# A hybrid encoder layer: the residual branch computed during attention and parked in DRAM

## The chip, the cores and the metric

The kernel runs on one core of one Trainium2 chip. The metric is the device time of one execution in microseconds, lower being better. The core's engines are named as in the profile: PE (matrix multiply), PEld (its weight loads), DVE (vector), ACT (activation), POOL (GpSimd) and SP (the engine that here issues DMAs).

## The reference, cut to what matters

One encoder layer over 1024 tokens of width 1024. The input is layer-normalised, projected by a 1024 x 6688 matrix, and read by two parallel groups: a bidirectional state-space scan (16 heads) and a differential attention (8 heads, two softmax maps each). Both outputs go through one output projection, and the normalised input is added back:

```python
h = layer_norm(x, ln_emb_g, ln_emb_b)
proj = h @ w_in                       # z, xbc, dt, q, k, v, g
...                                   # y_ssm from z, xbc, dt;  y_attn from q, k, v, g
mix = concatenate([y_ssm, y_attn]) @ w_out
out = layer_norm(ALPHA * h + mix, ln_g, ln_b)
```

The change is about the term `ALPHA * h`, called the residual or skip path below. Everything is float32; products are made from split high and low parts, three matmuls for one.

## The kernel before, in words

The program is one long straight line, woven by a planner (`Loom`, L47) from generators called lanes. Each lane yields what it must wait for; the planner keeps an estimate of each engine's time and, at each step, resumes the lane that could go first, ties being decided by the rank in `LANES` (L29). The order of the PE's instructions is fixed by that weave. The framework under it places the instructions of the other engines, each engine being an in-order queue.

The stages, by time in the profile: up to 90 us the input is normalised and transposed; to 450 us the state-space groups run beside the input projection; to about 1000 us the eight heads run (`scores`, `combine`, `values`, `finish`) while the rest of the input projection fills the PE (`fill`); the last head then runs beside the first half of the output projection (`project_out`, part 0), and from about 1110 us only the output projection, the final normalisation and the stores are left.

Names that the change and the prediction touch:

- `values` (L1033) writes each half head's output into the tile `o`, two buffers; `finish` (L1070) normalises and gates it and stores it to DRAM.
- `combine` (L1016) makes the map `p0*rs + p1*rs'`: a scaling on POOL (on ACT for the last head), then one two-input DVE instruction, listed as `p<-p,rs,p`.
- `rows_out` (L1137) loads row tiles `ws` of `w_out` and splits them into `oh`/`or` (ACT) and `ol`/`or` (POOL and DVE in turn).
- `y_out` (L1167) reads the concatenated outputs back as `ys` and splits them into `oyh` (ACT) and `oyl` (DVE).
- `residuals` (L1189) starts once the pool `ow` is open, after the projections of the last head. For each of 8 token tiles and 2 halves it loads `x` into `xr` and runs one ACT and two POOL instructions on it, plus one small `nmr` on DVE for each token tile.
- `project_out` (L1245) adds the residual to its PSUM banks (`bk`), which it shares with the transposes of `values`.
- `z_block` (L466) and `proj_k` (L909) each end in a DMA issued from SP: `zd<-zs` (16 times) and `kk<-kk` (32 times).

Of the kernel before, what the change touches and what calls it, by code (L numbers as in the profile page):

```python
# [9 lines left out]
F32 = mybir.dt.float32  # L10
# [9 lines left out]
D = 1024  # L20
# [5 lines left out]
EPS = 1e-5  # L26
ALPHA = 2.0 ** 0.25

LANES = dict(weights=(0, 0.8), channels=(1, 1.2), steps=(2, 1.6), z_tail=(2, 0.8), conv=(3, 1), v_tail=(3, 0.4), states=(4.4, 0.8), diag=(4.125, 0.6), maps=(4.4, 0.6), gate=(4.375, 0.2), finish=(4.2, 2), scores=(4, 0.8), combine=(4.125, 0.6), values=(4.25, 0.4), fill=(9, 0.8), rows_out=(9, 0.2), y_out=(9, 3), residuals=(9, 2), project_out=(9, 2))  # L29


def col_bcast(ap, n):
# [184 lines left out]
def hybrid_layer_kernel(  # L217
# [13 lines left out]
    VO = Engine(loom, nc.vector, "DVE", _dve_cost, pinned=True)  # L231
    AO = Engine(loom, nc.scalar, "ACT", _act_cost, pinned=True)
    SP = Engine(loom, nc.sync, "DMA", _dma_cost)
    x, out = x[0], out[0]
    w_in, w_out, conv_w = w_in[0], w_out[0], conv_w[0]

# [12 lines left out]

    def dma(dst, src):  # L250
        SP.dma_start(dst, src)

    def transpose(dst, src, n=128):
        T.transpose(dst, src, ident[:n, :n])
# [109 lines left out]
    y_dram = [dr.tile([128, 16, 128], F32, name=f"yd{k}") for k in range(8)]  # L364
    acs_dr = [dr.tile([16, NCH, 128], F32, name=f"acs_d{d}") for d in range(2)]
    zd = [dr.tile([NCH, 128, 512], F32, name=f"zd{g}") for g in range(2)]


    g0x = px.enter_context(ExitStack())
# [96 lines left out]
    def z_block(g, j, when=None):  # L466
        def evac(half, ps):
            zr = late["sq"].tile([128, 512], F32, name="zr", bufs=2)
            A.copy(zr, ps)

            def tail():
                pt = bank((128, 4, 128))
                yield (zr, pt)
                for i in range(4):
                    transpose(pt[:, i, :], zr[:, 128 * i:128 * i + 128])
                zs = late["sq"].tile([128, 4, 128], F32, name="zs", tag="zr", bufs=2)
                A.activation(zs, pt, AF.Silu)
                dma(zd[g][4 * half:4 * half + 4, :, 128 * j:128 * j + 128].rearrange("c p n -> p c n"), zs)
                G[g].z_done += 1
            loom.add(tail(), "z_tail")  # L480
        queue.append(Block(Z0 + 512 * g + 128 * j, evac, when))
# [427 lines left out]
    def proj_k(h):  # L909
        H = heads_[h]  # L910

        def evac(half, ps):
            if half == 0:
                H.kk = H.pool().tile([128, 2, S], F32R, name="kk")
                H.kl = H.pool().tile([128, S], F32R, name="kl")
            t = slice(512 * half, 512 * half + 512)
            for m in range(2):
                a, b = slice(64 * m, 64 * m + 64), slice(64 - 64 * m, 128 - 64 * m)
                A.copy(H.kk[a, m, t], ps[a])
                V.tensor_sub(H.kl[a, t], ps[a], H.kk[a, m, t].bitcast(F32))  # L920
                dma(H.kk[b, m, t].bitcast(F32), H.kk[a, m, t].bitcast(F32))
            H.k += 1
        queue.append(Block(K0 + 128 * h, evac, free_since(h, "scored", 8)))

# [108 lines left out]
    def values():  # L1033

        for _ in range(64):
            yield lambda: bool(maps_)
            H, tb, w = maps_.pop(0)
            if tb % 2 == 0:
                wh = ap.tile([128, NCH, 256], F32R, name="wh")
                wl = ap.tile([128, NCH, 256], F32R, name="wl")  # L1040
            t = slice(128 * (tb % 2), 128 * (tb % 2) + 128)
            for half in range(2):
                pt = bank((128, 4, 128))
                yield (w, pt)
                for j in range(4):
                    s = 4 * half + j
                    transpose(pt[:, j, :], w[:, 128 * s:128 * s + 128])
                b = slice(4 * half, 4 * half + 4)
                A.copy(wh[:, b, t], pt)
                yield wh  # L1050
                V.tensor_sub(wl[:, b, t], pt, wh[:, b, t].bitcast(F32))
            count["t"] += 1
            if tb % 2 == 0:
                continue
            yield lambda: H.v == 2
            if tb % 4 == 1:
                H.o = ap.tile([128, 512], F32, name="o", bufs=2)
            po = bank()
            yield (wl, H.vl, po)
            for s in range(NCH):  # L1060
                T.matmul(po[:, 0:256], H.vh[:, s, :], wh[:, s, :], start=(s == 0), stop=False)
                T.matmul(po[:, 0:256], H.vh[:, s, :], wl[:, s, :], start=False, stop=False)
                T.matmul(po[:, 0:256], H.vl[:, s, :], wh[:, s, :], start=False, stop=(s == NCH - 1))
            n = tb // 2 % 2
            A.copy(H.o[:, 256 * n:256 * n + 256], po[:, 0:256])
            H.summed += 1
            if n:
                loom.add(finish(H, H.o, tb // 4))
# [32 lines left out]
    for h in range(1, 8):  # L1101
        project_head(h)
    queue[-2].pair = queue[-1].last = True
    for lane in (scores, combine, values):
        loom.add(lane())


# [29 lines left out]
    def rows_out():  # L1137

        yield lambda: h_used[0] > 0
        order = [(k, n) for k in range(16) for n in range(2)]  # L1140
        sts = []

        def load():
            k, n = order[len(sts)]
            sts.append(ap.tile([128, 512], F32, name="ws", bufs=10))
            dma(sts[-1], w_out[128 * k:128 * k + 128, 512 * n:512 * n + 512])
        for _ in range(10):
            load()
        for places in (early_rows(), late_rows()):
            for p in places:  # L1150
                if callable(p):
                    yield p
                    continue
                k, n = order[sum(len(w) for w in wo)]
                st, (hi, lo) = sts[2 * k + n], p
                A.copy(hi, st)
                (V if n else P).tensor_sub(lo, st, hi.bitcast(F32))
                wo[k].append(p)
                if len(sts) < 32:
                    load()  # L1160
                if sum(len(w) for w in wo) == 32:
                    return
# [4 lines left out]
    def y_out():  # L1167

        for tb, part in units:
            if part == 0:  # L1170
                yield lambda: h_used[1] > 0 and len(ahead) < 2
            else:
                yield lambda: last.done == 2 and len(ahead) < 2
            parts = []
            for i in range(2):
                st = wp.tile([128, 4, 128], F32, name="ys", tag="wst", bufs=2)
                dma(st, y_dram[tb][:, 8 * part + 4 * i:8 * part + 4 * i + 4, :])
                hi = wp.tile([128, 4, 128], F32R, name="oyh", tag="whi", bufs=4)
                lo = wp.tile([128, 4, 128], F32R, name="oyl", tag="wlo", bufs=4)
                A.copy(hi, st)  # L1180
                V.tensor_sub(lo, st, hi.bitcast(F32))
                parts.append((hi, lo))
            ahead[tb, part] = parts

    res = {}
    used = set()
    halves = [slice(0, 512), slice(512, 1024)]

    def residuals():  # L1189

        yield lambda: "pool" in res
        for n, src in (("g", ln_emb_g), ("b", ln_emb_b)):
            res[n] = res["pool"].tile([128, D], F32, name=n + "_e")
            dma(res[n], src.partition_broadcast(128))
            A.activation(res[n], res[n], AF.Copy, scale=ALPHA)
        late = [("zr", 2), ("zr", 2), ("o", 2), ("o", 2), ("osq", 1), ("msq", 1)]
        for tb in range(8):
            yield lambda: tb < len(used) + 2 or tb > NE
            if tb == NE:
# [1 line left out]
            if tb > NE:  # L1201
                yield lambda: last.done == 2
            xr = []
            nmr = ap.tile([128, 1], F32, name="nmr", bufs=2)
            V.scalar_tensor_tensor(nmr, mv[tb][:, 0:1], -1.0, rstd[tb], op0=ALU.mult, op1=ALU.mult)
            for n, t in enumerate(halves):
                if tb < NE:
                    xr.append(res["pool"].tile([128, 512], F32, name=f"xr{tb}_{n}"))
                else:
                    tag, bufs = late[2 * (tb - NE) + n]  # L1210
                    xr.append(ap.tile([128, 512], F32, name="xr", tag=tag, bufs=bufs))
                dma(xr[n], x[128 * tb:128 * tb + 128, t])
                A.activation(xr[n], xr[n], AF.Identity, scale=rstd[tb], bias=nmr)
                P.tensor_mul(xr[n], xr[n], res["g"][:, t])
                P.tensor_add(xr[n], xr[n], res["b"][:, t])
            res[tb] = xr
        for n, src in (("g", ln_g[0]), ("b", ln_b[0])):
            res[n + "o"] = res["pool"].tile([128, D], F32, name=n + "_o", tag=n + "_e")
            dma(res[n + "o"], src.partition_broadcast(128))

    def norm_out(tb, xr, po, final):
        st = ap.tile([128, 2, 6], F32, name="bst", bufs=2)
# [96 lines left out]
```

## Time and profile before

| | us |
|---|---|
| median of 3 runs (1234.08 to 1236.62) | 1236.25 |
| the profiled execution, its own time | 1231.77 |
| its span, first to last instruction | 1230.1 |
| PE busy in the span | 1173.1 |

All times of rows are microseconds from the start of the span unless marked ns. A busy time is the union of an engine's instructions; the bracket at the end of a timeline line is the idle time before it and what ended it. Nearly all instructions show line L140, a helper's, so they are told apart by the names of tiles: `p<-p,rs,p` writes `p` and reads `p`, `rs` and `p`.

### The profile page before, as it was taken

Reading aid. Unit: us, or ns where it says so; the run is one execution under the profiler, and the core shown is the slowest. Engines: PE = TensorE matmul, PEld = TensorE weight load, DVE = VectorE, ACT = ScalarE, POOL = GpSimd, SP = SyncE. Lnnn points to the kernel's source line nnn. Section 1 sums busy time; section 2 is a strip of 40 time slices with the busy share of each in tenths; the row PEclk is TensorE's granted clock in tenths of the full one; section 3 lists DMA queues with packets and bytes.
Section 4 is the critical chain, followed back from the end, with each engine's and each line's share of the span. In section 5 each row is a group of like instructions: output and inputs, shape, how many; then the busy total and the mean of one; then the engine's idle time right before and its main releaser. Section 6 shows DMA issues by size and latency. Waiting matters only on the chain. (4 is left out here: it accounts for less than half of the span.)

```text
span 1230.1 us, 16472 instructions
## 1 busy us (share of the span) xinstructions
PE 1173.1 (95%) x5881; PEld 920.5 (75%) x5881; DVE 898.5 (73%) x1303; ACT 701.8 (57%) x1281; POOL 471.2 (38%) x404
## 2 busy tenths in 40 slices
PE   5999999999999999999999999999999997999997
PEld 3777667788668777778787777877777776788885
DVE  6686876767876568788788887887878888762334
ACT  4557578734577466566655657556656686552221
POOL 7412564323753223323332333233232429352354
PEclk9999999999899999999999999999999999999999
DMA  6113345622344531111111121121111263023221
GB/s 199 30 36 112 86 129 158 185 64 65 94 122 144 153 113 43 28 47 48 26 48 39 43 53 26 35 52 36 43 35 43 79 210 116 26 77 121 78 86 60
DMA packets 107590, 98.02 MB, mean 80 GB/s; under 512 B 9364, under 2 KB 79349, under 8 KB 107509
## 3 DMA queue, kind: packets, MB, share of 16 engines
q1 hardware_dynamic: 107509, 96.98, 27.4%
q8 instruction: 46, 0.75, 0.3%
q14 instruction: 35, 0.29, 0.1%
HBM read 75.85 MB, written 16.91 MB: 75 GB/s over the span
## 5 line engine op out<-in xcount | busy, mean ns | idle before, releaser
L140 PE MATMUL bk<-hh,whi 128*128 128x512 f32 x832 | 352.8, 424 | 0.9 <-DVE yt L140 0.3
L140 PE MATMUL bk<-hl,whi 128*128 128x512 f32 x832 | 327.2, 393 | 3.2 <-POOL hl L140 2.8
L140 PE MATMUL bk<-hh,wlo 128*128 128x512 f32 x832 | 328.2, 394 | 0.0
L140 ACT ACTIVATE p<-p,nm 128x1024 f32<-128x1024 f32 x128 | 146.8, 1148 | 127.7 <-DVE nm L140 126.9
L140 POOL TENSOR_TENSOR wlo<-wst,whi 128x512 fp32r<-128x512 f32 x104 | 159.0, 1534 | 144.6 <-ACT whi L140 122.2
L140 POOL TENSOR_SCALAR p<-p,rs 128x1024 f32<-128x1024 f32 x56 | 64.4, 1150 | 352.7 <-DVE rs L140 293.0
L140 PEld LDWEIGHTS bk<-hh,wlo 128*128 128x128 f32 x832 | 156.7, 188 | 35.0
L140 PEld LDWEIGHTS bk<-hh,whi 128*128 128x128 f32 x832 | 157.6, 189 | 33.1 <-issue 5.7
L140 PEld LDWEIGHTS bk<-hl,whi 128*128 128x128 f32 x832 | 157.8, 190 | 32.8 <-POOL hl L140 5.5
L140 DVE CUSTOM_DVE_ANT_0 p<-sc,dist 128x1024 f32<-128x1024 f32 x128 | 151.3, 1219 | 20.2 <-PE sc L140 19.6
L140 DVE SCALAR_TENSOR_TENSOR p<-p,rs,p 128x1024 f32<-128x1024 f32 x64 | 127.7, 1995 | 21.3 <-POOL p L140 18.0
L140 ACT CAST wh<-bk 128x512 fp32r<-128x512 f32 x128 | 74.2, 580 | 50.5 <-PE bk L140 49.9
L140 DVE TENSOR_TENSOR wl<-bk,wh 128x512 fp32r<-128x512 f32 x128 | 87.1, 684 | 15.6 <-ACT wh L140 13.6
L140 ACT CAST whi<-wst 128x512 fp32r<-128x512 f32 x104 | 64.1, 621 | 42.5 <-PE bk L140 34.3
L140 PE MATMUL bk<-ident,p 128*128 128x128 f32 x512 | 78.3, 275 | 2.6 <-ACT o L140 2.2
L140 PEld LDWEIGHTS bk<-ident,p 128*128 128x128 f32 x512 | 61.0, 140 | 26.1 <-issue 5.5
L140 ACT ACT_TABLE_LOAD x46 | 59.0, 1283 | 28.9 <-DVE t L140 17.3
L140 PE MATMUL bk<-wh,vh 128*128 128x256 f32 x256 | 74.7, 292 | 0.0
L140 PE MATMUL sc<-kk,q 128*128 128x512 f32 x256 | 72.3, 394 | 0.0
L140 PE MATMUL bk<-wl,vh 128*128 128x256 f32 x256 | 72.0, 281 | 0.0
L140 PE MATMUL bk<-wh,vl 128*128 128x256 f32 x256 | 72.0, 281 | 0.0
L140 PEld LDWEIGHTS bk<-xt,t 128*128 128x128 f32 x256 | 45.0, 190 | 24.7 <-issue 16.0
(217 smaller groups left out, 2161.3 us busy)
## 6 DMA issues: line engine op xcount, KB each, us to landing
wst<-in_w_in_dram SPq DMA_DIRECT2D x104, 256.0 KB, 3.0
t<-acs_d SPq DMA_DIRECT2D x64, 256.0 KB, 3.4
ws<-in_w_out_dram SPq DMA_DIRECT2D x32, 256.0 KB, 3.8
ys<-yd SPq DMA_DIRECT2D x32, 256.0 KB, 3.0
xb<-in_x_dram SPq DMA_DIRECT2D x8, 512.0 KB, 6.5
zd<-zs SPq DMA_DIRECT2D x16, 256.0 KB, 3.0
gz<-zd SPq DMA_DIRECT2D x16, 256.0 KB, 3.1
yd<-ys SPq DMA_DIRECT2D x16, 256.0 KB, 2.8
```

Source lines behind the costliest of these rows:

```text
L140: r = f(*args, **kw)
```

## The change

- A new lane `skip_rows` computes the residual during attention. It runs a burst after each of eight half heads (the second to the ninth `o` tile). A burst has two tiles of 128 x 512: load `x`, one small DVE instruction, one ACT instruction, two on POOL, and, delayed by two tiles, a store to the new DRAM tensor `xr_dram`. The tiles are taken from the ring of `o`, which grows from two to four buffers. The scale and bias are loaded by halves.
- `residuals` now only loads `xr_dram` and, first, the last norm's scale and bias.
- `ws` goes from ten buffers to seven.
- For part 0, the first of the two `oyl` subtractions goes from DVE to POOL (8 instructions).
- The DMAs `zd<-zs` and `kk<-kk` are issued from ACT's queue in place of SP's.

```diff
-LANES = dict(... scores=(4, 0.8), ...)
+LANES = dict(... skip_rows=(3.9, 0), scores=(4, 0.8), ...)
...
+    AD = Engine(loom, nc.scalar, "DMA", _dma_cost)
+    def dma_act(dst, src):
+        AD.dma_start(dst, src)
+    xr_dram = [dr.tile([128, D], F32, name=f"xrd{b}") for b in range(NCH)]
...
-                dma(zd[g][4 * half:4 * half + 4, :, 128 * j:128 * j + 128].rearrange("c p n -> p c n"), zs)
+                dma_act(zd[g][4 * half:4 * half + 4, :, 128 * j:128 * j + 128].rearrange("c p n -> p c n"), zs)
...
-                dma(H.kk[b, m, t].bitcast(F32), H.kk[a, m, t].bitcast(F32))
+                dma_act(H.kk[b, m, t].bitcast(F32), H.kk[a, m, t].bitcast(F32))
...
-                H.o = ap.tile([128, 512], F32, name="o", bufs=2)
+                H.o = ap.tile([128, 512], F32, name="o", bufs=4)
+                o_turn[0] += 1
...
+    def skip_rows():
+        left = []
+        def store():
+            dst, t = left.pop(0)
+            dma(dst, t)
+        for i in range(8):
+            yield lambda: o_turn[0] > i + 1
+            for j in range(2):
+                n, tb = i // 4, 2 * (i % 4) + j
+                t = slice(512 * n, 512 * n + 512)
+                if tb == 0:
+                    for name, src in (("g", ln_emb_g), ("b", ln_emb_b)):
+                        resid[name] = ap.tile([128, 512], F32, name=name + "_e")
+                        dma(resid[name], src[t].partition_broadcast(128))
+                        A.activation(resid[name], resid[name], AF.Copy, scale=ALPHA)
+                if len(left) > 1:
+                    store()
+                xe = ap.tile([128, 512], F32, name="xe", tag="o", bufs=4)
+                dma(xe, x[128 * tb:128 * tb + 128, t])
+                nmr = ap.tile([128, 1], F32, name="nmr", bufs=2)
+                V.scalar_tensor_tensor(nmr, mv[tb][:, 0:1], -1.0, rstd[tb], op0=ALU.mult, op1=ALU.mult)
+                A.activation(xe, xe, AF.Identity, scale=rstd[tb], bias=nmr)
+                P.tensor_mul(xe, xe, resid["g"])
+                P.tensor_add(xe, xe, resid["b"])
+                left.append((xr_dram[tb][:, t], xe))
+        while left:
+            store()
...
-            sts.append(ap.tile([128, 512], F32, name="ws", bufs=10))
+            sts.append(ap.tile([128, 512], F32, name="ws", bufs=7))
...
-                V.tensor_sub(lo, st, hi.bitcast(F32))
+                (V if part or i else P).tensor_sub(lo, st, hi.bitcast(F32))
...
-            nmr = ap.tile([128, 1], F32, name="nmr", bufs=2)
-            V.scalar_tensor_tensor(nmr, mv[tb][:, 0:1], -1.0, rstd[tb], op0=ALU.mult, op1=ALU.mult)
...
-                dma(xr[n], x[128 * tb:128 * tb + 128, t])
-                A.activation(xr[n], xr[n], AF.Identity, scale=rstd[tb], bias=nmr)
-                P.tensor_mul(xr[n], xr[n], res["g"][:, t])
-                P.tensor_add(xr[n], xr[n], res["b"][:, t])
+                dma(xr[n], xr_dram[tb][:, t])
```

## Rows read from the trace of the kernel before

**Rows 1.** The page's first part: busy us, share of the span, instructions.
```profile
PE 1173.1 (95%) x5881; PEld 920.5 (75%) x5881; DVE 898.5 (73%) x1303; ACT 701.8 (57%) x1281; POOL 471.2 (38%) x404
```
**Rows 2.** Windows: length, busy PE, PEld, DVE, ACT, POOL, then clock, DMA share, GB/s.
```profile
90.00:450.00 360.00, 340.83 (x1613) 261.80 (x1612) 257.99 (x335) 221.33 (x473) 148.33 (x132) 0.99 0.41 121
490.00:770.00 280.00, 278.90 (x1503) 220.09 (x1502) 224.87 (x338) 174.05 (x303) 85.92 (x64) 1.00 0.16 39
1000.00:1065.00 65.00, 57.65 (x280) 45.44 (x279) 52.48 (x71) 45.88 (x73) 44.03 (x31) 0.95 0.39 127
...
1110.00:1222.00 112.00, 112.00 (x484) 90.61 (x482) 37.79 (x72) 22.31 (x33) 46.96 (x39) 1.00 0.28 86
```
**Rows 3.** Timeline of PE from 1000 to 1065: the matmuls after idle time.
```profile
1020.22 0.50 PE L140 MATMUL bk<-oh,oyh 128*128 128x512 f32 x1 [2.47 <-DVE wl L140]
1040.71 1.39 PE L140 MATMUL bk<-oh,oyh 128*128 128x512 f32 x2 [3.91 <-DVE wl L140]
1064.23 0.50 PE L140 MATMUL bk<-oh,oyh 128*128 128x512 f32 x1 [0.97 <-DVE xr L140]
```
**Rows 4.** Windows, columns as in rows 2, behind the second gap.
```profile
1040.70:1042.00 1.30, 1.28 (x3) 0.89 (x4) 1.30 (x3) 0.00 (x0) 1.22 (x2) 0.50 0.00 0
...
1046.00:1048.00 2.00, 2.00 (x9) 1.09 (x8) 0.00 (x0) 0.00 (x0) 2.00 (x2) 0.86 0.00 0
```
**Rows 5.** Timeline of DVE ahead of the first gap's end.
```profile
1015.36 2.40 DVE L140 TENSOR_TENSOR oyl<-ys,oyh 128x512 fp32r<-128x512 f32 x2
...
1018.34 1.22 DVE L140 TENSOR_TENSOR rs<-rs,neg_lam 128x1 f32<-128x1 f32 x1
1019.48 0.68 DVE L140 TENSOR_TENSOR wl<-bk,wh 128x512 fp32r<-128x512 f32 x1
```
**Rows 6.** Timelines of ACT and of DVE ahead of the second gap's end.
```profile
1035.91 2.91 ACT L140 ACTIVATE xr<-xr,nmr,rstd 128x512 f32<-128x512 f32 x4
1038.73 0.56 ACT L140 CAST wh<-bk 128x512 fp32r<-128x512 f32 x1
...
1036.56 2.28 DVE L140 SCALAR_TENSOR_TENSOR p<-p,rs,p 128x1024 f32<-128x1024 f32 x1
1038.77 1.29 DVE L140 SCALAR_TENSOR_TENSOR nmr<-mv,rstd 128x1 f32<-128x1 f32 x2
1039.98 0.68 DVE L140 TENSOR_TENSOR wl<-bk,wh 128x512 fp32r<-128x512 f32 x1
```
**Rows 7.** Tile xr: duration ns min/median/max, first and last start us, forms.
```profile
L140 ACT ACTIVATE xr<-xr,nmr,rstd x16: 798/808/819, 1017.3 to 1119.5; 128x512 f32<-128x512 f32 x16
L140 POOL TENSOR_TENSOR xr<-xr,g_e x16: 1266/1298/2279, 1018.2 to 1120.4; 128x512 f32<-128x512 f32 x16
L140 POOL TENSOR_TENSOR xr<-xr,b_e x16: 1278/1298/2123, 1019.6 to 1121.8; 128x512 f32<-128x512 f32 x16
```
**Rows 8.** Windows of tile xr alone: length, busy DVE, ACT, POOL, clock, DMA.
```profile
1000.00:1065.00 65.00, 3.70 (x6) 8.87 (x12) 34.41 (x24) 0.95 0.39 127
```
**Rows 9.** Tiles rs, p, oyl, o and ws, columns as in rows 7.
```profile
L140 DVE TENSOR_TENSOR rs<-rs,neg_lam x64: 151/160/1223, 436.5 to 1082.8; 128x1 f32<-128x1 f32 x64
L140 DVE SCALAR_TENSOR_TENSOR p<-p,rs,p x64: 1268/2296/2340, 437.8 to 1085.8; 128x1024 f32<-128x1024 f32 x64
...
L140 DVE TENSOR_TENSOR oyl<-ys,oyh x32: 676/684/1795, 990.7 to 1200.3; 128x512 fp32r<-128x512 f32 x32
...
L140 ACT COPY o<-bk x32: 346/352/373, 460.8 to 1098.5; 128x256 f32<-128x256 f32 x32
...
L140 ACT CAST oh<-ws x16: 617/622/637, 971.2 to 1012.8; 128x512 fp32r<-128x512 f32 x16
```
**Rows 10.** Tiles zs and kk: the DMA issues, columns as in rows 7.
```profile
L140 SPq DMA_DIRECT2D zd<-zs x16: 359/371/508, 122.4 to 388.3; - x16
...
L140 SPq DMA_DIRECT2D kk<-kk x32: 461/467/777, 406.3 to 964.3; - x32
```
**Rows 11.** Waits of SP's queue, 90 to 450: us in total, times, longest.
```profile
SPq L140 <- ACT zs L140: 27.0, 11, 7.1
```

More of the change, by code (lines that the diff above doesn't have):

```diff
@@ L27 @@
 ALPHA = 2.0 ** 0.25
-LANES = dict(weights=(0, 0.8), channels=(1, 1.2), steps=(2, 1.6), z_tail=(2, 0.8), conv=(3, 1), v_tail=(3, 0.4), states=(4.4, 0.8), diag=(4.125, 0.6), maps=(4.4, 0.6), gate=(4.375, 0.2), finish=(4.2, 2), scores=(4, 0.8), combine=(4.125, 0.6), values=(4.25, 0.4), fill=(9, 0.8), rows_out=(9, 0.2), y_out=(9, 3), residuals=(9, 2), project_out=(9, 2))
+LANES = dict(weights=(0, 0.8), channels=(1, 1.2), steps=(2, 1.6), z_tail=(2, 0.8), conv=(3, 1), v_tail=(3, 0.4), states=(4.4, 0.8), diag=(4.125, 0.6), maps=(4.4, 0.6), gate=(4.375, 0.2), finish=(4.2, 2), skip_rows=(3.9, 0), scores=(4, 0.8), combine=(4.125, 0.6), values=(4.25, 0.4), fill=(9, 0.8), rows_out=(9, 0.2), y_out=(9, 3), residuals=(9, 2), project_out=(9, 2))
 def col_bcast(ap, n):
@@ L1103, in hybrid_layer_kernel @@
     queue[-2].pair = queue[-1].last = True
-    for lane in (scores, combine, values):
+    resid = {}
+    o_turn = [0]
+    def skip_rows():
[25 more added lines that the diff above has]
+            store()
+    res = {}
+    for lane in (scores, combine, values, skip_rows):
         loom.add(lane())
@@ L1144, in load @@
             k, n = order[len(sts)]
-            sts.append(ap.tile([128, 512], F32, name="ws", bufs=10))
+            sts.append(ap.tile([128, 512], F32, name="ws", bufs=7))
             dma(sts[-1], w_out[128 * k:128 * k + 128, 512 * n:512 * n + 512])
-        for _ in range(10):
+        for _ in range(7):
             load()
@@ L1180, in y_out @@
                 A.copy(hi, st)
-                V.tensor_sub(lo, st, hi.bitcast(F32))
+                (V if part or i else P).tensor_sub(lo, st, hi.bitcast(F32))
                 parts.append((hi, lo))
             ahead[tb, part] = parts
-    res = {}
     used = set()
@@ L1191, in residuals @@
         yield lambda: "pool" in res
[L1192 to L1196, printed above, removed]
+        for n, src in (("g", ln_g[0]), ("b", ln_b[0])):
+            res[n + "o"] = res["pool"].tile([128, D], F32, name=n + "_o")
+            dma(res[n + "o"], src.partition_broadcast(128))
+        late = [("zr", 2), ("zr", 2), ("o", 4), ("o", 4), ("o", 4), ("o", 4)]
         for tb in range(8):
@@ L1211, in residuals @@
                     xr.append(ap.tile([128, 512], F32, name="xr", tag=tag, bufs=bufs))
-                dma(xr[n], x[128 * tb:128 * tb + 128, t])
-                A.activation(xr[n], xr[n], AF.Identity, scale=rstd[tb], bias=nmr)
-                P.tensor_mul(xr[n], xr[n], res["g"][:, t])
-                P.tensor_add(xr[n], xr[n], res["b"][:, t])
+                dma(xr[n], xr_dram[tb][:, t])
             res[tb] = xr
-        for n, src in (("g", ln_g[0]), ("b", ln_b[0])):
-            res[n + "o"] = res["pool"].tile([128, D], F32, name=n + "_o", tag=n + "_e")
-            dma(res[n + "o"], src.partition_broadcast(128))
     def norm_out(tb, xr, po, final):
```

## The prediction

> **What bounds the kernel now.** I read the page's first part first: PE is busy 95% of the span [rows 1], so only PE's idle time and a lower clock can be won back: the change takes no matmul away. Then windows by stage [rows 2]. In 490 to 770, attention with projections filling in, PE is busy 278.90 of 280 us, while DVE has 224.87, ACT 174.05 and POOL 85.92: there is room beside PE, most of it on POOL. In 1110 to 1222, where the output projection stands alone, PE is busy 112.00 of 112: nothing done for the other engines there can pay. In 1000 to 1065, the last head beside the output projection, PE is busy 57.65 of 65 and its clock averages 0.95. That is the stretch to look at, and it is also where the residual runs.
>
> Third, the gaps in PE's timeline there: 2.47, 3.91 and 0.97 us [rows 3]. The first two end when DVE has written `wl`, which frees the PSUM bank that the output projection wants; the third ends with the addition of a residual, `xr`. Behind the 3.91 us gap PE comes back at a granted clock of 0.50, 1.2 GHz in place of 2.4, and in the window from 1046 to 1048 it averages 0.86 [rows 4]. So half speed lasted 5.3 us to 1046 and 0.56 us more (0.14 of 2 us, over 0.50), and half of these 5.9 us, 2.9 us, were lost. The 2.47 us gap had no such window behind it.
>
> Fourth, what made `wl` late, in the queues of ACT and DVE.
>
> - First gap: DVE spent 2.40 us on two `oyl`, then 1.22 us on an `rs` of 128x1 before `wl` [rows 5]. The same `rs` has a median of 160 ns [rows 9]. POOL was in a residual instruction at that moment.
> - Second gap: on ACT four activations of `xr` took 2.91 us, and only then came the cast `wh`; on DVE the combination `p<-p,rs,p` took 2.28 us, and a pair of the residual's `nmr` 1.29 us, before `wl` could start at 1039.98 [rows 6]. The combination takes 1268 ns at its shortest [rows 9].
>
> POOL is busy 44.03 us in this stretch [rows 2], 34.41 of them with `xr` [rows 8]. So the residual crowds the last head twice: directly on ACT, and through POOL's effect on DVE.
>
> **The change, part by part.**
>
> *Residual work taken out of the end.* It is 16 x 0.808 us on ACT and 32 x 1.298 us on POOL [rows 7], 12.9 and 41.5 us, of which 8.87 and 34.41 us fall in 1000 to 1065 [rows 8]. What PE gets:
>
> - First gap, 2.47 us: `rs` falls back from 1.22 to 0.16 us (1.06), and one of the two `oyl`, 0.68 us at its median, goes to POOL. Left: 2.47 - 1.06 - 0.68 = 0.73; gain 1.7 us.
> - Second gap, 3.91 us: ACT reaches `wh` 2.91 us earlier. DVE gains 1.0 us on `p` and 1.29 us on `nmr`, 2.3 us here, and has shorter instructions ahead as well, so I let ACT's 2.9 us decide. A gap of 1.0 us is left, shorter than the two that kept the clock, so the 2.9 us of half speed go too. Gain 5.8 us; bounds 2.3 us (DVE binds and the clock still falls) and 6.8 us (all of it).
> - Third gap: nothing computes `xr` any more; gain 1.0 us.
>
> Sum 8.5 us, from 5.0 to the 10.3 us of gaps and clock that the stretch has.
>
> *The same work put into attention.* A burst follows each of eight half heads. The 32 copies to `o`, two for a half head, run from 460.8 to 1098.5 [rows 9], so a half head lasts some 40 us, and the bursts lie between about 500 and 790. A burst costs 4 x 1.3 = 5.2 us on POOL and 1.6 us on ACT. Over 280 us POOL goes from 85.92 to about 127, ACT from 174 to 187; both are covered by PE's 278.90 us of matmuls. If that cover were gone, the scaling of a map on POOL would come up to 5.2 us late eight times, then `p`, then PE's transposes: 41.5 us. Below, the bound is zero, since PE has only 1.1 us of idle time to win there. DVE holds the middle: `p<-p,rs,p` is at 2.3 us in the median against 1.27, so this DVE instruction already pays for POOL's company without PE waiting. I take the value near zero, 0.2 us for a burst, 1.6 us in all, because the rows nearest to it are the attention's own.
>
> The row shows the price of company: up to 1.0 us for one DVE instruction [rows 9]. The Trainium skill (SBUF — State Buffer, Who interferes with whom) goes further: a DVE instruction with two SBUF inputs and a GpSimd instruction that reads SBUF exclude each other for their whole length, and whichever starts second blocks fully. By that rule the contention is moved with the work and not removed, and 32 instructions could hold DVE for 41.5 us, taking it from 224.87 to 266 of 280 us, still under PE.
>
> *Loads and stores.* 16 loads and 16 stores are new in attention, where the DMAs are 0.16 busy [rows 2]; the 16 loads at the end stay, of the same size. A load of `x` waits for a buffer of the `o` ring, and SP's queue with the weights stands behind it. The ring is full when a burst starts (two `o`, two stored tiles), but the older `o` is being finished and the first store is issued ahead of the load. I cost this at nothing under the same cover.
>
> *Seven `ws` buffers.* The 16 early casts `oh` spread over 41.6 us [rows 9], 2.6 us apiece on average. Row tile 8 now has to be reloaded after tile 1 is split, some seven steps earlier or 18 us. Nothing, with a bound of 2.5 us, the size of the first gap, if one reload comes late.
>
> *One `oyl` in four on POOL.* Eight times 0.68 us less on DVE, and 1.3 us more on POOL, 10.4 us in place of 41.5. Counted above.
>
> *48 DMAs on ACT's queue.* At the durations of SP's issues [rows 10], 16 x 0.371 + 32 x 0.467 = 20.9 us move to ACT. Behind each DMA stands ACT's next instruction, and the DMA waits for the `zs` or `kk` that ACT itself has just written. In 90 to 450 ACT is busy 221.33 of 360 us. On the other side, SP no longer waits for `zs`, 27.0 us over 11 times [rows 11], with the loads behind it. PE waits for neither by name, so I take nothing, bounds 3 us better (a ninth of SP's waits) and 8 us worse (0.4 us for 16 `zs` and the first 4 `kk`). The Trainium skill (DMA: Bandwidth & Descriptors, Issuing engines are not separate DMA queues) says that a second issuing engine saves only the time to initiate a DMA. By that sentence SP would win 20.9 us of issuing and the transfers nothing; the 27.0 us of waits show that a place in the queue can be worth more.
>
> *Sum.* -8.5 + 1.6 = -6.9 us. On the profiled execution that gives 1231.8 - 6.9 = 1224.9. This execution ran 4.5 us under the median of the runs, so against the median I say 1236.25 - 6.9 = **1229.3 us**. The forecast's own range runs from 1225 to 1233.
>
> **The rivals.** A difference of 0.2%, 2.5 us, is about what a measurement of this kernel can tell from none.
>
> 1. *Attention pays (slower).* A residual's POOL instruction lands ahead of a map's scaling, and the cover is thinner than 1.1 us of idle time suggests: a full PE may have no spare work in its fixed order when `p` is late. It decides from 8.5 / 16 = 0.53 us of PE for each tile. At one POOL instruction, 1.3 us a tile, the price is 20.8 us: 1236.25 - 8.5 + 20.8 = 1248.6. For it: `p` at 2.3 us. Against it: no idle time of PE there. Chance 0.12. The Trainium skill's rule of full exclusion on the page SBUF — State Buffer is this rival's side of the argument.
> 2. *ACT's queue pays in the scan (slower to same).* The 20 DMAs before 450 cost PE 8 us: 1229.3 + 8 = 1237.3. There PE has 19 us of idle time already, so lateness shows. Against: ACT has 139 us free. Chance 0.09; half of it slower by the bound.
> 3. *The gaps stay.* The last head is late for its own splits (`ol`, `oyl`) and another wait takes the place: only 1 to 2 us are won, 1234.5 to 1236. For it: two of DVE's slow instructions ahead of the first gap are not the residual's. Chance 0.14.
> 4. *More than forecast.* The relieved last head also loses its remaining gaps, and SP's shorter waits give 3 us: 1236.25 - 10.3 - 3 = 1223. Chance 0.08.
>
> **How the numbers follow.** The forecast has 0.57. Faster: 0.57 + 0.08 = 0.65. Slower: 0.12 + 0.05, and 0.04 of a weave that comes out worse after 450 from rival 3's share, 0.21. The rest, 0.14, is within the bound. The range takes in rival 4 from below and rivals 2 and 3 above, and leaves most of rival 1 out: 1222 to 1240.
>
> **What would show it.** Right: windows of 1000 to 1065 with PE over 63 us busy and no clock of 0.50, POOL under 25 us there, and attention with PE still over 99%. Wrong: gaps of PE between 500 and 790 that end with `p` or `wl`, at the bursts; longer waits of PE for `t`, `H` or `xc` before 450; or gaps at the end that now wait for `oyl` on POOL or for `ws`.

## The result, and the profile after

The changed kernel takes 1250.33 us (median of 4 runs, 1246.17 to 1253.76); the kernel before took 1235.16 on the same chip. The ratio is 1.0122, interval 1.0101 to 1.0142: slower by 15 us, where 1229.3 and faster had been forecast, and outside the range. The profiled execution has a span of 1246.4 us, 16.3 longer than before.

Windows, columns as in rows 2; the first line is of the kernel before, the others of the changed one:

```profile
490.00:960.00 470.00, 468.31 (x2527) 370.43 (x2526) 378.58 (x567) 289.19 (x505) 143.37 (x107) 1.00 0.16 39
...
90.00:450.00 360.00, 337.33 (x1588) 259.12 (x1589) 258.19 (x333) 220.27 (x472) 148.31 (x132) 0.98 0.41 120
490.00:770.00 280.00, 272.84 (x1462) 217.83 (x1461) 218.28 (x329) 176.48 (x301) 117.63 (x87) 1.00 0.24 67
490.00:960.00 470.00, 460.92 (x2474) 368.52 (x2474) 365.14 (x553) 292.71 (x503) 176.49 (x132) 1.00 0.22 58
960.00:1000.00 40.00, 33.97 (x188) 26.65 (x186) 35.82 (x49) 30.29 (x53) 22.25 (x15) 0.97 0.37 113
1000.00:1065.00 65.00, 57.56 (x287) 44.01 (x287) 46.97 (x77) 33.49 (x56) 9.12 (x7) 0.91 0.36 113
```

The work went where it should: POOL falls from 44.03 us to 9.12 in 1000 to 1065 and rises from 85.92 to 117.63 in attention [rows 2]. PE has nothing of it. The last stretch still has 57.56 busy of 65, at a lower clock (0.91 for 0.95), and attention, full before, now has 7.2 us of idle time in 280.

PE's timeline after, its matmuls behind some of the larger idle times from 490 to 1045:

```profile
527.87 0.50 PE L140 MATMUL bk<-osl,ones_r 128*128 128x512 f32 x1 [1.46 <-DVE osl L140]
...
608.31 0.38 PE L140 MATMUL bk<-wl,vh 128*128 128x256 f32 x1 [1.06 <-DVE wl L140]
...
722.04 0.63 PE L140 MATMUL bk<-ident,p 128*128 128x128 f32 x4 [1.39 <-DVE p L140]
...
996.12 0.50 PE L140 MATMUL bk<-osl,ones_r 128*128 128x512 f32 x1 [1.93 <-DVE osl L140]
...
1000.09 0.79 PE L140 MATMUL bk<-oh,oyh 128*128 128x512 f32 x1 [2.86 <-DVE wl L140]
...
1034.78 1.22 PE L140 MATMUL bk<-ident,p 128*128 128x128 f32 x8 [3.46 <-DVE p L140]
...
1038.10 0.79 PE L140 MATMUL bk<-osh,ones_r 128*128 128x512 f32 x1 [2.11 <-DVE wl L140]
```

The end has gaps like those of [rows 3], with other names and at other places in the program. Two engines ahead of the 3.46 us gap, first DVE, then POOL:

```profile
1028.30 1.23 DVE L140 CUSTOM_DVE_ANT_0 p<-sc,dist 128x1024 f32<-128x1024 f32 x1 [0.28 <-PE sc L140]
...
1032.24 0.16 DVE L140 TENSOR_TENSOR rs<-rs,neg_lam 128x1 f32<-128x1 f32 x1
1033.34 1.28 DVE L140 SCALAR_TENSOR_TENSOR p<-p,rs,p 128x1024 f32<-128x1024 f32 x1 [0.95 <-ACT p L140]
```

```profile
1021.49 1.12 POOL L140 TENSOR_SCALAR p<-p,rs 128x1024 f32<-128x1024 f32 x1 [7.65 <-DVE rs L140]
1033.91 1.85 POOL L140 TENSOR_TENSOR o<-o,gate 128x512 f32<-128x512 f32 x1 [11.30 <-ACT osq L140]
```

Nothing crowds the head here. POOL has been idle for 11.30 us, `p<-p,rs,p` runs at its shortest (1.28 us), `rs` takes 0.16. PE waits out one head's own chain, from scores to map, and has nothing else in its order to do meanwhile. So the question became why the order has nothing there. The tile `o` after:

```profile
L140 ACT COPY o<-bk x32: 346/372/373, 465.6 to 1114.9; 128x256 f32<-128x256 f32 x32
```

There are two of these copies for each half head, 32 in all. (The expectations below call each of them a half head.) The first starts 4.8 us later than before and the last 16.4 later [rows 9]; but the 25th, read from ACT's timeline, starts at 972.18 in place of 939.37, 32.8 later. PE's idle time explains 4.8 + 7.4 of that (9.1 idle in 490 to 960 against 1.7). The rest is matmuls that had come later. Counted in the program's order of PE, the matmuls of the input projection (2,528 in all, `bk<-hh,whi` and the like) that stand ahead of the last matmul that a copy waits for:

```
end of copy to `o`       8    12    16    24    26    27
before                1544  1736  1928  2312  2414  2471
changed               1568  1799  2003  2405  2504  2528
```

By the 24th copy, 93 projections have been pulled ahead of the scores. In PE's timeline, 146 still start behind the 25th copy before and 52 after; the 94 between are 21 us at 0.227 us from one to the next: 4.8 + 7.4 + 21 = 33 us. By the end of the 27th all are used up, where the kernel before has 57 left.

### The profile page after: what moved, and what is told of

Same layout as the page of the kernel before. It is cut to its first block, busy times and chain, and to the rows that moved or that the text cites. A ratio compares the mean times of both kernels' runs of the same rounds, so it can differ in the third digit from the quotient of the medians.

```text
span 1246.4 us, 16472 instructions
## 1 busy us (share of the span) xinstructions
PE 1174.2 (94%) x5881; PEld 924.2 (74%) x5881; DVE 887.4 (71%) x1303; ACT 706.3 (57%) x1283; POOL 479.0 (38%) x412
## 5 line engine op out<-in xcount | busy, mean ns | idle before, releaser
L140 POOL TENSOR_TENSOR wlo<-wst,whi 128x512 fp32r<-128x512 f32 x104 | 155.9, 1502 | 172.5 <-ACT whi L140 166.7
L140 DVE SCALAR_TENSOR_TENSOR p<-p,rs,p 128x1024 f32<-128x1024 f32 x64 | 107.4, 1678 | 19.5 <-POOL p L140 14.9
L140 PE MATMUL bk<-ident,p 128*128 128x128 f32 x512 | 78.1, 276 | 10.7 <-DVE p L140 6.6
```

What stands on the lines that cost most here:

```text
L140: r = f(*args, **kw)
```

## The experiments

Theory A, rival 1 of the prediction: the residual's instructions make the attention's chain late. Theory B, formed from the counts above: the planner counts the lane's work on ACT, POOL and DVE and writes another order for PE, which leaves the last heads without cover. Theory C: a queue, ACT's with the 48 DMAs or SP's with the last norm's rows in front.

A table for reading along. PE's loss between 490 and 1065 is worked out from windows: idle time in three of them, and for the last (1 - clock) x 65 us. The profiled execution is one of each kernel's runs, so losses and medians agree only to some us; that of "work, not told", 1247.98, is the slowest of its 7 runs. Each ratio stands against runs of the kernel before on the same chip.

| kernel | idle 490-960 | 960-1000 | 1000-1065 | clock | loss | median us | ratio to before |
|---|---|---|---|---|---|---|---|
| before | 1.7 | 3.4 | 7.4 | 3.3 | 15.6 | 1235.16 | |
| DMAs on ACT alone | 0.6 | 2.2 | 6.0 | 3.3 | 12.1 | 1232.72 | 0.9988 (0.9975 to 1.0000) |
| no work on the tile | 0.6 | 2.3 | 2.7 | 0 | 5.5 | 1231.26 | 0.9965 (0.9949 to 0.9981) |
| told of it, no work | 6.1 | 5.5 | 6.7 | 4.6 | 22.8 | 1245.12 | 1.0074 (1.0051 to 1.0097) |
| work, not told | 10.7 | 0 | 5.2 | 0 | 15.8 | 1240.71 | 1.0060 (1.0037 to 1.0084) |
| changed | 9.1 | 6.0 | 7.4 | 5.9 | 28.4 | 1250.33 | 1.0122 (1.0101 to 1.0142) |
| spread | 7.2 | 2.7 | 2.4 | 0 | 12.3 | 1238.87 | 1.0037 (1.0024 to 1.0050) |
| spread, no POOL | 0.9 | 2.2 | 1.9 | 2.0 | 7.1 | 1228.50 | 0.9950 (0.9932 to 0.9968) |
| spread, no ACT | 3.1 | 3.2 | 2.0 | 0 | 8.3 | 1231.43 | 0.9974 (0.9962 to 0.9987) |

The table leaves out the clock ahead of 1000. It was 0.99 in 490 to 960 in "work, not told" and in "spread": half speed behind two gaps each, which adds some 3.4 us to their loss. And it was 0.96 in 960 to 1000 in the three kernels with 2.2 or 2.3 us there, 1.6 us more each (0.97 in the changed kernel, 1.2 us). Over the whole span PE is busy 1174.2 us after and 1173.1 before [rows 1], so some 15 of the span's 16.3 us are idle time of PE.

**1. Only the DMAs on ACT's queue, in the kernel before.**

```diff
-dma(zd[...], zs)    -dma(H.kk[...], H.kk[...])
+dma_act(zd[...], zs)    +dma_act(H.kk[...], H.kk[...])
```

> The kernel before with one part of the change alone: the 16 zd stores and 32 kk copies are issued from ACT's queue. PE's order is that of before. If ACT's queue is what costs the 4 us that PE is late by 430 us in the changed kernel, this one is 4 us slower than before or more (1239 us and up), with the transposes of the first v block at 430 in place of 426. If it is not, 1233 to 1237.

1232.72, no difference that could be told with certainty. Theory C's first half doesn't explain 15 us.

**2. The changed kernel with these DMAs back on SP's queue.** The reverse edit.

> The changed kernel with those 48 DMAs back on SP's queue, PE's order unchanged. By the theory of ACT's queue 4 us faster than the changed kernel or more (1246 and below); by the theories that put the loss into the order of the weave or into the work in attention 1249 to 1252.

1257.11, 1.0185 (1.0164 to 1.0206), slower than both ranges expected: 6.8 us over the changed kernel, so here ACT's queue helps. SP's waits of this kernel from 90 to 1000 have a line that the changed kernel lacks:

```profile
SPq L140 <- ACT kk L140: 50.9, 18, 10.2
```

**3. The same DMAs one kind at a time, in the kernel before.**

> The kernel before with only the 16 zd stores on ACT's queue. In the run with both, PE was 4.4 us late at 430 and made it up by the end. If the zd stores on ACT cause the lateness, it stays here: 1236 to 1239. If not, as before, 1232 to 1235.

> The kernel before with only the 32 kk copies on ACT's queue. If the kk copies on ACT are what made up 4 us during the heads and cost nothing earlier, 1228 to 1231; if the time is only shifted by chance, 1232 to 1235.

`zd` alone: 1237.85, 1.0024 (1.0011 to 1.0037), with PE busy 333.84 of 360 in 90 to 450 against 340.83 [rows 2]. `kk` alone: **1230.15**, 0.9962 (0.9950 to 0.9973). It beats the kernel before and the changed one. The null of experiment 1 is two effects of opposite sign.

**4. The last norm's rows loaded behind the residual.** The three lines of the loop over `ln_g` and `ln_b` in `residuals` move behind the loop over the token tiles.

> The changed kernel with the loads of the last norm's scale and bias put behind the loads of the residual again, as before. In the changed kernel SP stands 14.1 us at the first of them, for memory that head 6 still uses, and the loads of ys behind it come late. If that wait starves the output projection, its matmuls fill the stretch from 1016 to 1043 and the kernel takes 1242 to 1246; if another load takes the place at the head of the queue, or the output projection has nothing to do there anyway, 1249 to 1252.

1245.96, 1.0107 (1.0083 to 1.0131): 4.4 us under the changed kernel by the medians, but with intervals that overlap. SP's queue does wait there in the changed kernel, for a buffer that the last heads still read (its waits, 960 to 1080):

```profile
SPq L140 <- PE bk L140: 17.4, 2, 14.1
```

But with the rows out of the way PE's gaps from 996 to 1038 stayed, 58.56 busy of 65 at clock 0.92. The queue isn't what empties PE there.

**5. The lane's ACT, POOL and DVE instructions left out.**

```diff
-nmr = ap.tile([128, 1], F32, name="nmr", bufs=2)
-V.scalar_tensor_tensor(nmr, ...)
-A.activation(xe, xe, AF.Identity, scale=rstd[tb], bias=nmr)
-P.tensor_mul(xe, xe, resid["g"])
-P.tensor_add(xe, xe, resid["b"])
```

> The changed kernel with the lane's ACT instruction, its two POOL instructions and its DVE instruction left out: x is loaded and stored as it is, so the output lacks the first norm in the residual. PE's order is that of before up to the last head. If the engines' work is what costs, the gaps at osl in 490 to 770 vanish and it takes 1230 to 1235, the gain at the end remaining. If the loads and stores on SP's queue or the ring of o cost by themselves, gaps remain there and it takes 1238 or more.

1231.26, 19.1 us under the changed kernel. Its windows:

```profile
490.00:960.00 470.00, 469.41 (x2546) 373.87 (x2545) 386.67 (x572) 290.04 (x503) 150.98 (x106) 1.00 0.22 57
...
1000.00:1065.00 65.00, 62.34 (x322) 49.05 (x321) 48.51 (x74) 43.66 (x74) 16.65 (x11) 1.00 0.42 136
```

Attention is full again and the relief at the end is there. Loads and stores of the tiles, four `o` and seven `ws` are innocent of the gaps. But PE's order went back to that of before as well (2312 at the 24th copy), so A and B are not yet apart. It is that of before for the first 5,022 of 5,881 matmuls, to 1032 us here; in the last head the transposes of `p` and the output projection then alternate otherwise. So the relief at the end is that of less work and of this other order together.

**6. The work without telling the planner.** The lane's instructions are issued directly, not through the engines' wrappers that count their cost.

```diff
-A.activation(xe, ...)
-P.tensor_mul(xe, xe, resid["g"])
+nc.scalar.activation(xe, ...)
+nc.gpsimd.tensor_mul(xe, xe, resid["g"])
```

and so for the addition and for the lane's loads of `x` and its stores; `nmr` and the loads of scale and bias stay counted.

> The changed kernel, but the planner is not told of the new lane's loads, ACT, POOL and store instructions (they are issued all the same), so it plans the matmuls as if attention had no more to do. If the loss lies in the order that the weave chose, with projections ahead of scores, head 6 ends some 25 us earlier and the kernel takes 1238 to 1243. If the work itself is what holds attention (POOL's company for DVE, ACT's time), the gaps between 490 and 770 stay at 6 us or grow and it takes 1249 or more.

1240.71, 9.6 us under changed. PE's order is that of experiment 5, matmul for matmul, and still PE waits in attention (waits of PE, 490 to 960):

```profile
PE bk L140 <- DVE osl L140: 9.5, 7, 2.5
```

Six of the seven are 0.95 to 1.45 us. The longest is at 620.22, behind the burst whose POOL instructions ran from 598.22 to 604.4. What DVE did ahead of it, and then the same two instructions in experiment 5:

```profile
616.19 2.31 DVE L140 SCALAR_TENSOR_TENSOR p<-p,rs,p 128x1024 f32<-128x1024 f32 x1
618.42 1.75 DVE L140 TENSOR_TENSOR osl<-osq,osh 128x512 fp32r<-128x512 f32 x1
```

```profile
603.85 2.31 DVE L140 SCALAR_TENSOR_TENSOR p<-p,rs,p 128x1024 f32<-128x1024 f32 x1 [1.13 <-POOL p L140]
606.09 1.78 DVE L140 TENSOR_TENSOR osl<-osq,osh 128x512 fp32r<-128x512 f32 x1
```

The durations are the same. But `osl` starts 1.1 us behind PE's matmul on `osh` (617.31) here, and 1.5 us ahead of it (607.59) there. These two are late, not longer.

What made them late stands further up, and there some instructions are longer. DVE, POOL and ACT, at the burst itself:

```profile
599.25 1.25 DVE L140 SCALAR_TENSOR_TENSOR nmr<-mv,rstd 128x1 f32<-128x1 f32 x1
...
601.01 0.84 DVE L140 SCALAR_TENSOR_TENSOR nmr<-mv,rstd 128x1 f32<-128x1 f32 x1
```

```profile
598.22 2.25 POOL L1141 TENSOR_TENSOR xe<-xe,g_e 128x512 f32<-128x512 f32 x1
600.55 1.28 POOL L1142 TENSOR_TENSOR xe<-xe,b_e 128x512 f32<-128x512 f32 x1
```

```profile
606.48 0.63 ACT L140 ACTIVATE g_e<-g_e 128x512 f32<-128x512 f32 x1 [1.61 <-DMA g_e<-in_ln_emb_g_dram]
```

The lane's `nmr` ends within 0.03 us of a POOL instruction of the lane each time (600.47 and 601.83), and without POOL's work it takes 0.15 us in the median (experiment 12). And ACT stood 1.61 us at the reload of the residual's scale, `g_e`: it has one buffer, its DMA was issued at 603.12 when POOL had read the first half for the last time (603.09), and the head's next map stood behind it on ACT. In the changed kernel ACT is idle for 5.11 us ahead of the same reload. Where POOL's work is left out (experiment 5) both go: nothing reads the first half, and the second is loaded by 450. So the price of the work includes a longer `nmr` and this reload, which no run splits off.

**7. The planner told of the work, and the work left out.** Experiment 5 with four notes of cost in place of the instructions.

```diff
+loom.note("DVE", _dve_cost("scalar_tensor_tensor", ...), ...)
+loom.note("ACT", _act_cost("activation", ...), ...)
+loom.note("POOL", _pool_cost("tensor_mul", ...), ...)
+loom.note("POOL", _pool_cost("tensor_add", ...), ...)
```

> The run without any work on the tile again (the residual is neither normalised nor scaled), but the planner counts the lane's DVE, ACT and POOL instructions as if they were issued, so PE's projections run ahead of the scores as in the changed kernel (2405 before the 24th half head, not 2312). If the order costs by itself, 1238 to 1243 with PE idle and the clock at half around 1030; if the order costs only together with the work, 1230 to 1234.

1245.12, slower than before (and than expected) without one instruction of the residual's arithmetic on the tiles. PE's order is that of the changed kernel, matmul for matmul, and so are its gaps at the end; PE's timeline:

```profile
995.28 0.49 PE L140 MATMUL bk<-osl,ones_r 128*128 128x512 f32 x1 [1.80 <-DVE osl L140]
...
999.25 0.80 PE L140 MATMUL bk<-oh,oyh 128*128 128x512 f32 x1 [2.86 <-DVE wl L140]
...
1033.12 1.94 PE L140 MATMUL bk<-ident,p 128*128 128x128 f32 x8 [3.47 <-DVE p L140]
```

This shows B. (The notes change the whole weave; the runs don't split PE's order from that of the other engines.) Experiments 5 to 7 and the changed kernel are a square: over the 1231.26 with neither, the order alone costs 13.9 us, the work alone 9.4, both 19.1. By the ratios, each against the kernel before of its own session, it is 13.5, 11.7 and 19.4.

**8. The lane behind all others.** Rank 9 in place of 3.9: `skip_rows=(9, 0)`.

> The changed kernel with the new lane ranked last (9) in place of ahead of the scores (3.9). The planner still counts the lane's work, but PE's order up to the last head is then that of the kernel before. If the loss is the order of the weave alone, 1234 to 1240. If the work in attention costs by itself (about 1.4 us a burst at the matmul that waits for osl, as in the run with the blind planner), 1240 to 1245.

1261.1, 1.0211 (1.0181 to 1.0240), over both ranges. Attention was clean (469.39 busy of 470), but the lane starved; tile `xe`:

```profile
L140 POOL TENSOR_TENSOR xe<-xe,g_e x16: 1261/1283/1802, 986.2 to 1056.7; 128x512 f32<-128x512 f32 x16
```

All of the residual came to lie at the end, now with a way through DRAM on top: 1000 to 1065 has PE at 44.29 of 65 and clock 0.79, with one gap of 8.60 us for an `oh`. So the lane must stand ahead of something to run early at all.

**9. The lane's POOL work on DVE.** `P.tensor_mul` and `P.tensor_add` of the lane become `V.`.

> The changed kernel with the lane's two POOL instructions for each tile moved to DVE: 32 x 0.68 us there, none on POOL. PE's order drifts as in the changed kernel (2390 projection matmuls before the 24th half head against 2312 before the change). If POOL holding DVE's instructions is what costs in attention, the gaps between 490 and 960 fall under 3 us and it takes 1243 to 1247; if the drift of the order is what counts, 1247 to 1252.

1254.54, 1.0163 (1.0148 to 1.0177), over both ranges and no better than changed. Each instruction falls to 0.69 us from 1.30, and `nmr` to 0.15, but now DVE has them in its own queue. The drift stays (2390 projections at the 24th copy), and so do waits for `osl` (5.3 us) and `wl` (3.6) in attention.

**10. Sixteen bursts of one tile in place of eight of two.** One after every third map.

```diff
-for i in range(8):
-    yield lambda: o_turn[0] > i + 1
-    for j in range(2):
-        n, tb = i // 4, 2 * (i % 4) + j
+for i in range(16):
+    yield lambda: count["t"] > 3 * i + 5
+    for j in range(1):
+        n, tb = i // 8, i % 8
...
-if len(left) > 1:
+if left:
```

> The changed kernel with its bursts cut up: 16 bursts of one tile, one after every third map, in place of 8 bursts of two after every half head. All work stays in attention, and the planner is told of it; PE's order up to the last head is now that of the kernel before. If bunched work is what moved the weave and made osl late, 1231 to 1236 and no gap over 1 us between 490 and 960. If the work costs whatever its place, 1239 to 1244, as with the blind planner.

1238.87, 11.5 us under changed, just under the second range. With this placing the planner gives PE's order of experiment 5, so that of before up to the last head, although it counts the work. The end is relieved (62.56 of 65, clock 1.00). What is left is A's share, waits of PE in 490 to 960:

```profile
PE bk L140 <- DVE osl L140: 5.3, 5, 1.5
PE bk L140 <- DVE wl L140: 1.1, 1, 1.1
```

**11. The same with `zd` back on SP's queue and the last norm's rows late.**

> The same 16 single bursts, and two more parts undone: the zd stores are back on SP's queue (which cost 2.7 us on ACT by itself) and the last norm's rows are loaded behind the residual (4.4 us in the changed kernel). If these parts add up with the spread, 1224 to 1230, faster than before; if the SP wait mattered only while the weave left the output projection no work, only the 2.7 us are seen beside the run with the spread alone.

1235.49, 1.0001 (0.9990 to 1.0013) over 12 runs: the best found with all of the residual's work in attention, and no gain over the kernel before.

**12. Which engine's share it is.** Experiment 10 without the two POOL instructions, and without the ACT one.

> The kernel with 16 single bursts, its two POOL instructions for each tile left out (the residual is not scaled and shifted); ACT's instruction, the loads and stores stay. PE's order stays. If POOL holding DVE's two-input instructions is the cost in attention, the gaps at osl go and it takes 1230 to 1233, like the run without any work on the tile. If ACT's part or its wait for the load is the cost, 1236 to 1239.

> The same with ACT's instruction left out in place of POOL's two (the residual is not normalised). If POOL is the cost, 1236 to 1239 with the gaps at osl as in the run with the spread alone; if ACT is, 1230 to 1233.

1228.50, under its lower range, and 1231.43, against 1238.87 with both. By the expectations the first result points at POOL and the second at ACT. Windows, first without POOL's work, then without ACT's:

```profile
490.00:960.00 470.00, 469.06 (x2537) 373.09 (x2536) 387.38 (x584) 300.17 (x518) 154.80 (x108) 1.00 0.22 58
```

```profile
490.00:960.00 470.00, 466.93 (x2524) 370.83 (x2524) 383.75 (x569) 289.08 (x500) 197.32 (x135) 1.00 0.22 59
```

Taking out POOL's part wins 10.4 us, taking out ACT's 7.4, and all of it 7.6 (experiment 5). The parts don't add up. POOL's alone leaves 2.5 us of waits, ACT's alone 0.3.

The traces say more. First, both of the larger waits that POOL's work alone leaves stand behind the reload of `g_e` (ACT, then PE, without ACT's instruction):

```profile
712.81 0.63 ACT L140 ACTIVATE g_e<-g_e 128x512 f32<-128x512 f32 x1 [3.00 <-DMA g_e<-in_ln_emb_g_dram]
```

```profile
727.78 0.47 PE L140 MATMUL bk<-osh,ones_r 128*128 128x512 f32 x1 [1.12 <-DVE wl L140]
729.24 0.50 PE L140 MATMUL bk<-osl,ones_r 128*128 128x512 f32 x1 [0.98 <-DVE osl L140]
```

Second, each of the two edits also makes `nmr` harmless. Without ACT's instruction nothing holds it back, and all 16 run from 440.3 to 441.7, ahead of attention. Without POOL's work it is short; tile `nmr` from 450 to 1000, spread and then spread without POOL:

```profile
L140 DVE SCALAR_TENSOR_TENSOR nmr<-mv,rstd x14: 160/566/1245, 470.5 to 878.2; 128x1 f32<-128x1 f32 x14
```

```profile
L140 DVE SCALAR_TENSOR_TENSOR nmr<-mv,rstd x14: 144/154/420, 476.0 to 871.7; 128x1 f32<-128x1 f32 x14
```

In the spread kernel PE's gaps at `osl` of 528.37, 609.11, 689.01 and 853.37 come 18 to 19 us behind an `nmr` of 1.24 us or more; the tiles with 0.71 us or less have none, save the one with the reload. So a rival to "the work crowds the queues" is that one DVE instruction of 128x1 beside POOL, and the reload, are most of the price in single tiles. It is read from the traces and not tested: no run moves `nmr` ahead of attention or loads the whole scale at once. In bursts of two tiles it can't be all, for the last gap of experiment 6 (1.16 us at 784.98) has no `nmr` near it.

## Why the prediction was wrong

**The step that failed** is "The same work put into attention", taken at 0.2 us a burst, 1.6 us in all. It failed twice.

- *The size.* On an unchanged order of PE, the work costs 9.4 us (experiment 6 against 5; 11.7 by the ratios), and 7.6 in single tiles (8.9): 0.5 to 0.7 us of PE a tile. Rival 1 gave 0.53 as the point from which the sign turns. The argument was that PE was busy 278.90 of 280 us and the others had room. But a PE that is always busy isn't a PE with matmuls to spare: its order is fixed, and each `osl`, `wl` and `p` has its place in it. Behind seven of the eight bursts of 5.2 us on POOL and 1.6 on ACT it waited 1 to 2.5 us at the end of the half head (experiment 6). Average room (DVE 55 us free, ACT 106) said nothing on that. The sum also had no price for `nmr` beside POOL, though it had met one of 1.29 us for a pair [rows 6], nor for the reload of the scale on ACT's queue.
- *The order.* That the planner would write another order had no term, only 0.04 of the chances, without a price. It costs 13.9 us alone (experiment 7 against 5), more than the work by the medians; the intervals of the two runs overlap. The lane comes to PE's cover by way of the planner's estimates, without touching PE: 93 projections move ahead of the scores, the last heads stand alone, and the gaps and the lower clock of [rows 3, 4] come back under other names, though the residual is gone from there. That the estimates of ACT and POOL are what moves them is shown by the notes of experiment 7; which comparison in the planner tips was not tried.

**Relief at the end**, 8.5 us: right in place, roughly in size. Where the order is kept (experiment 5), the loss in 490 to 1065 falls from 13.7 us with the DMAs alone to 7.1, 6.6 us less, and from 15.6 in the kernel before, 8.5 less (the clock of 960 to 1000 counted in). Part of it may be the other order in the last head. The first gap left is 1.79 us where I had 0.73, and half speed is gone from 1000 to 1065 as predicted. But it comes once before: behind a gap of 2.25 us at 986.39 the clock was 0.50 from 988 to 991, while the gap of 2.47 us in the kernel before had kept full speed. That half speed goes when the gap gets shorter, as the prediction had it, is not borne out there. In the medians only 1.5 us of the relief is to be seen (1232.72 to 1231.26; 2.8 by the ratios). In the profiles the first copy to `o` starts 3.0 us later, at 468.59 against 465.59, and in kernels that share this beginning anywhere from 464.3 to 472.4. Whether the change costs something there is open.

**POOL's company on DVE** as the reason of the end's lateness: half right. `rs` and `p` are short in the last heads after. In attention `p` and `osl` paid for company already and got no longer (experiments 5 and 6), but `nmr` did. Experiment 9 doesn't decide what that is worth, for it puts 1.4 us a tile on DVE in place of the company. The Trainium skill (SBUF — State Buffer, Who interferes with whom) states that a DVE instruction with two SBUF inputs contends with a GpSimd instruction that reads SBUF, and that the port pair they share is an exclusive lock. The trace agrees on `nmr`, which has two SBUF inputs: in experiment 6 it ends at 600.50, POOL's instruction beside it at 600.47. How much of the 9.4 us that explains no run shows.

**The DMAs on ACT's queue**, zero with bounds of -3 and +8: the sum is right (-1.1 us in experiment 1), the reason isn't. `zd` costs 2.7 us, within the bounds; `kk` wins 5.0, beyond them, and both together are worth 6.8 us in the changed kernel. I had read SP's waits to 450 only, where `zs` stands out [rows 11], while the `kk` issues run on to 964 [rows 10]; SP's waits for `kk` before, in 90 to 1000, have the weights queued behind them:

```profile
SPq L140 <- ACT kk L140: 62.3, 16, 7.9
```

The Trainium skill (DMA: Bandwidth & Descriptors, Issuing engines are not separate DMA queues) allows only the time to initiate as a saving. That is 32 x 0.467 = 15 us of SP's time here; the runs don't split it from those waits.

**Loads and stores, seven `ws`, the larger ring**: nothing, as said (experiment 5), except the reload of the scale, which experiment 5 doesn't test. Of the signs named, POOL under 25 us in 1000 to 1065 came true; PE over 63 us there did not, and gaps at `p` and `wl` in attention, named for the case of a wrong forecast, appeared, with `osl` beside them.

**The rivals.** Rival 1's time, 1248.6, is near the result, but by luck: it has 20.8 us for the work, which costs 9.4 to 11.7, and no term for the order. Rival 2 happened in part (`zd`). Rival 3, the gaps stay, is what the changed kernel's last stretch shows, for a reason that it didn't give.

**Left open:** how much of the work's price is `nmr` and the reload, which would explain why POOL's and ACT's shares don't add up; and where in the profile the 5 us of `kk` arise: its profiled execution, 1232.18, is the slowest of its runs and shows no such gain.

## What to carry to other kernels

A bottleneck engine that is busy all the time under a fixed order has no cover to give away: before moving work beside it, look how late each result that it waits for could come, not how much time the other engines have; count the small instructions and reloads that go along with the work, too. Where a planner writes the order, adding work to any engine is a change to the bottleneck's order; compare the two orders first, and separate the two by one kernel with the work and not the estimate and one with the estimate and not the work. Move queue entries one kind at a time, since a null can be a gain and a loss.

## What the runs showed of the hardware that I had not expected

Issuing from ACT costs what it costs from SP. Tile `kk` after, its issues and landings:

```profile
L140 ACTq DMA_DIRECT2D kk<-kk x32: 468/468/521, 408.7 to 957.0; - x32
DMA to landing us min/median/max: 2.2/2.2/3.9
```

From SP the issue took 467 ns [rows 10], and the landing, in the kernel before:

```profile
DMA to landing us min/median/max: 2.3/3.2/3.4
```

In the median the `kk` copies thus landed 1.0 us sooner after their issue, with the same bytes (0.9 with `kk` alone moved, 2.3 us). And a DVE instruction on one column, 128x1, took 0.15 us in the median without the lane's POOL work and up to 1.25 us beside it (experiment 12).
